# A hybrid attention and GLA layer on one core: more buffers for raw weights, deferred transposes, scalings on ScalarE, and modulation steps moved

## The chip, the cores and the metric

The kernel runs on one core of a Trainium2 chip. A core has TensorE (PE, matrix products; its weight loads are listed apart as PEld), VectorE (DVE), ScalarE (ACT), GpSimd (POOL) and SyncE (SP), which here issues most transfers. Each engine works through its own queue in order. The metric is the device time of one execution in microseconds (us).

## The reference

One layer of a diffusion backbone, batch 1, 256 latent tokens x and 256 context tokens, model width 2048, all in 32-bit floats:

```python
mod = silu(c) @ w_mod + b_mod            # 6 parts of 2048: shift1, scale1, gate1, shift2, scale2, gate2
h = rms_norm(x, g_mix) * (1 + scale1) + shift1           # the context tokens with c_ctx
qa, ka, va, qb, kb, vb, rb, lr_f, lr_b, gate_a, gate_b = split(h @ w_in)
# attention: 16 query heads, 4 key heads of 128; q and k normalised per head, rotary, window 128, sink
o_attn = softmax_with_sink(q @ k.T * 128**-0.5, [window, context]) @ v
# GLA: 4 heads (keys 256, values 512), forward and backward, decay from lr_f and lr_b
o_gla = gla_forward + gla_backward
y = sigmoid(gate_a) * (o_attn @ w_attn_o) + sigmoid(gate_b) * ((rms_norm(o_gla) * silu(rb)) @ w_gla_o)
x = x + gate1 * (y @ w_out)
h2 = rms_norm(x, g_ffn) * (1 + scale2) + shift2
a, g = split(conv3(h2 @ w_up))           # depthwise convolution over tokens, width 3; 2 x 5632 wide
out = x + gate2 * ((silu(a) * g) @ w_down)
```

## The kernel before

**Projections.** Every float matrix product is made of three products of fp32r operands: both operands are split into an upper half (hi) and the rest (lo), and hi x hi, hi x lo and lo x hi are summed. Weights are read once, in chunks of 256 rows and 512 columns (512 KB). `wload` (line 137) takes a raw buffer from the pool `wr`, which has four, and has SP load the chunk. `wsplit` (143) makes `whi` on ScalarE (line 61) and `wlo` on VectorE (line 62), each with three buffers; a raw buffer is free when wlo is made. `proj_nat` (152) gives tokens by features, 512 columns a product (lines 163 to 165), with two accumulator banks for the latent tokens or four with the context; `proj_T` (169) gives features by tokens, 256 columns a product (lines 186 to 189). There are four accumulator banks. When a block of 512 features is done, a function called evac takes the banks away.

**Work beside the projections.** Each chunk begins with a `tick` (124). It runs steps of a generator (`beside`: the GLA of a head, or an attention group) and of a list of background steps, `bg_steps`, each at a pace set by the program. The background list is the modulation of the later parts (`mod_latent`, 225): a step loads a 512 KB piece of w_mod into a raw buffer and adds two row tiles, scaled by silu(c), to a sum on VectorE (line 239, `macc`); every eighth step closes 512 columns with a transpose, a reduction and a small product (line 247, `pcl`). Parts 3, 4, 2 and 5 (shift2, scale2, gate1, gate2) are 32 steps each.

**Stages.** First the inputs are normalised, the modulation parts 0 and 1 are computed, and h is made in five groups of row tiles, with the first projections (to about 236 us). Then the four GLA heads run beside the remaining key and value projections of GLA (`gla_A`, 460; to 500). Then come the attention's keys KA and values VA (to 600; `ka_evac`, 676, normalises, rotates and transposes each bank of four heads), four query blocks QA with the attention of the group before beside each (`qa_block`, 689; `attend`, 702; to 800), the GLA output blocks RB and the merge (`rb_evac`, 784; `mg_evac`, 818; `to_T`, 776; to 1200), the output projection (`wo_evac`, 838; to about 1300), and the FFN: up-projection, convolution and down-projection in two halves (6 and 5 blocks). `norm_rope` (653) is the per-head norm: copy and square on ScalarE, sum on VectorE, `rms_scale` (276, seven tiny instructions on both), scaling and rotation on VectorE. `rows_from_cols` (257) turns a gate into rows in every partition by way of memory, with transfers on POOL's queue. The pace of background steps is 0.7 a tick during GLA, 2.0 during KA and VA, 0 during QA, 0.5 from RB on.

**What sets the order.** A scheduler orders each engine's instructions when the kernel is built, by the program's order, priorities (wsplit is preferred) and its own estimates of time, and puts in the waits. From then on every queue runs in that order.

## Time and profile before

| | |
|---|---|
| median of 3 runs | 2062.91 us (2056.2 to 2065.13) |
| the profiled execution: span, first to last instruction | 2061.8 us |
| busy: PE, PEld, DVE, ACT | 97%, 84%, 68%, 45% of the span |
| granted TensorE clock, mean | 0.990 |
| moved from and to memory | 413.71 MB, mean 201 GB/s |

For the profiled execution the profile gives the span; it lies 1.1 us under the median of the runs, and what lies around it is taken as that. The table of stages gives for each stretch the busy time of each engine with the count of its instructions, the granted clock (1.00 is full), the share of time that the 16 transfer engines were busy, and GB/s. A row of waits reads: engine, what waited, who released it, then us in total, times, and the longest. PE's busy time overstates its work, since neighbouring products overlap and a product that waits for its operand may count as busy.

### The profile page before, as it was taken

The page shows a single profiled execution, that of the slowest core. Times are in us where ns is not written, and L with a number is a line of the kernel's source. Part 1 is how long each engine was busy: PE and PEld are TensorE (multiplying, and loading weights), DVE is VectorE, ACT ScalarE, POOL GpSimd, SP SyncE. Part 2 cuts the span into 40 slices and gives each one's busy share as a digit, 9 for nine tenths or more (in the row PEclk, how much of TensorE's full clock was granted, in tenths as well). Part 3 has the DMA queues.
Part 4 walks back from the last instruction along what each step waited for, and adds up shares of the span by engine and source line. Part 5 has one row for each costly group of instructions (what it writes and reads, how often), then busy time and mean ns, then how long its engine had stood idle before and what let it go on. Part 6 is the DMA issues. An engine that isn't in the chain of part 4 may idle for free.

```text
span 2061.8 us, 30115 instructions
## 1 busy us (share of the span) xinstructions
PE 1999.2 (97%) x11792; PEld 1721.8 (84%) x11792; DVE 1405.7 (68%) x2149; ACT 937.4 (45%) x1306; POOL 41.9 (2%) x62
## 2 busy tenths in 40 slices
PE   6899999999999999999999999899999999999999
PEld 4679888888787777777787788899999889999987
DVE  4666778978867888777767665666666555666654
ACT  3323464552346665443334344554455334445533
POOL 0001100001000000000000000000000000000000
PEclk8999999999999999999999999999999999999999
DMA  9976434347664466787888875566666566666664
GB/s 347 337 247 197 120 111 123 113 118 226 213 186 114 121 194 192 254 270 260 264 279 272 294 235 184 164 184 184 184 183 184 194 193 187 184 184 183 183 209 150
DMA packets 214350, 413.71 MB, mean 201 GB/s; under 512 B 12548, under 2 KB 21092, under 8 KB 213184
## 3 DMA queue, kind: packets, MB, share of 16 engines
q1 hardware_dynamic: 212320, 406.89, 63.3%
q0 software_dynamic: 1360, 4.74, 0.8%
q8 instruction: 92, 1.51, 0.3%
q14 instruction: 50, 0.41, 0.1%
q10 hardware_dynamic: 528, 0.17, 0.0%
HBM read 409.63 MB, written 2.11 MB: 200 GB/s over the span
## 4 chain that ended last, share of the span: by engine, by line
PE 60%; issue 18%; DMA 11%; DVE 8%; ACT 2%; POOL 0%; DVEq 0%; ACTq 0%; POOLq 0%
PE acc L189 10%; PE acc L186 10%; PE acc L188 10%; PE acc L165 8%; PE acc L164 8%; PE acc L163 8%; DMA raw<-in_w_mod 8%; DVE wlo L62 3%; DVE macc L239 2%; DMA raw<-in_w_in 2%; PE pm L210 1%; PE pa L503 1%; ACT whi L61 1%; DMA raw<-in_w_gla_o 1%; PE po L589 1%
## 5 line engine op out<-in xcount | busy, mean ns | idle before, releaser
L61 ACT ACTIVATE whi<-raw 128x1024 fp32r<-128x1024 f32 x568 | 601.4, 1059 | 863.7 <-PE acc L165 366.4
L62 DVE TENSOR_TENSOR wlo<-raw,whi 128x1024 fp32r<-128x1024 f32 x568 | 693.3, 1222 | 428.3 <-ACT whi L61 422.7
L186 PE MATMUL acc<-h2h,whi 128*128 128x256 f32 x1408 | 399.5, 284 | 1.3 <-ACT h2h L346 1.3
L188 PE MATMUL acc<-h2l,whi 128*128 128x256 f32 x1408 | 399.5, 284 | 0.0
L189 PE MATMUL acc<-h2h,wlo 128*128 128x256 f32 x1408 | 399.2, 284 | 0.0
L186 PEld LDWEIGHTS acc<-h2h,whi 128*128 128x128 f32 x1408 | 271.3, 193 | 1.9 <-ACT h2h L346 1.8
L188 PEld LDWEIGHTS acc<-h2l,whi 128*128 128x128 f32 x1408 | 271.3, 193 | 0.2
L189 PEld LDWEIGHTS acc<-h2h,wlo 128*128 128x128 f32 x1408 | 271.3, 193 | 0.0
L239 DVE SCALAR_TENSOR_TENSOR macc<-raw,ccol,macc 128x512 f32<-128x512 f32 x240 | 180.6, 752 | 100.5 <-DMA raw<-in_w_mod 97.2
L163 PE MATMUL acc<-whi,h01hi 128*128 128x512 f32 x352 | 139.5, 396 | 0.9 <-ACT whi L61 0.9
L164 PE MATMUL acc<-wlo,h01hi 128*128 128x512 f32 x352 | 139.1, 395 | 1.3 <-DVE wlo L62 1.2
L163 PE MATMUL acc<-whi,h00hi 128*128 128x512 f32 x352 | 139.2, 395 | 0.0
L164 PE MATMUL acc<-wlo,h00hi 128*128 128x512 f32 x352 | 139.0, 395 | 0.2 <-DVE wlo L62 0.2
L165 PE MATMUL acc<-whi,h00lo 128*128 128x512 f32 x352 | 138.6, 394 | 0.0
L165 PE MATMUL acc<-whi,h01lo 128*128 128x512 f32 x352 | 138.2, 392 | 0.0
L163 PE MATMUL acc<-whi,ah 128*128 128x512 f32 x352 | 137.0, 389 | 0.0
L164 PE MATMUL acc<-wlo,ah 128*128 128x512 f32 x352 | 137.0, 389 | 0.0
L165 PE MATMUL acc<-whi,al 128*128 128x512 f32 x352 | 136.9, 389 | 0.0
L164 PEld LDWEIGHTS acc<-wlo,h01hi 128*128 128x128 f32 x352 | 66.4, 189 | 16.0 <-DVE wlo L62 3.2
L163 PEld LDWEIGHTS acc<-whi,h01hi 128*128 128x128 f32 x352 | 66.4, 189 | 14.3 <-ACT whi L61 1.3
L164 PEld LDWEIGHTS acc<-wlo,h00hi 128*128 128x128 f32 x352 | 66.2, 188 | 14.1 <-DVE wlo L62 1.3
L165 PEld LDWEIGHTS acc<-whi,al 128*128 128x128 f32 x352 | 66.1, 188 | 13.8
(369 smaller groups left out, 3393.2 us busy)
## 6 DMA issues: line engine op xcount, KB each, us to landing
raw<-in_w_in SPq DMA_DIRECT2D x208, 512.0 KB, 4.2
raw<-in_w_up SPq DMA_DIRECT2D x176, 512.0 KB, 3.7
raw<-in_w_mod SPq DMA_DIRECT2D x128, 512.0 KB, 3.9
raw<-in_w_down SPq DMA_DIRECT2D x88, 512.0 KB, 3.8
mraw<-in_w_mod SPq DMA_DIRECT2D x32, 1024.0 KB, 10.2
raw<-in_w_attn_o SPq DMA_DIRECT2D x32, 512.0 KB, 4.8
raw<-in_w_gla_o SPq DMA_DIRECT2D x32, 512.0 KB, 5.2
raw<-in_w_out SPq DMA_DIRECT2D x32, 512.0 KB, 3.8
```

What stands on the lines that cost most here:

```text
L61: S.activation(hi, src, AF.Copy)
L62: V.tensor_tensor(lo, src, hi.bitcast(F32), op=ALU.subtract)
L163: PE.matmul(banks[i], ahi, hi[:, k, :], start=(kt == kts[0]), stop=False)
L164: PE.matmul(banks[i], ahi, lo[:, k, :], start=False, stop=False)
L165: PE.matmul(banks[i], alo, hi[:, k, :], start=False, stop=(kt == kts[-1]))
L186: PE.matmul(o, whi, ahi, start=(kt == kts[0] and b == 0), stop=False, skip_group_check=True)
L188: PE.matmul(o, whi, alo, start=False, stop=False, skip_group_check=True)
L189: PE.matmul(o, wlo, ahi, start=False, stop=(kt == kts[-1]), skip_group_check=True)
L210: PE.matmul(a[0][q:q + 32, :], cS[:, kt, :], raw[:, k, :], start=(kt < 4), stop=(kt >= 12))
L239: V.scalar_tensor_tensor(a[0], raw[:, k, :], ccol[:, kt:kt + 1], a[0], op0=ALU.mult, op1=ALU.add)
L503: PE.matmul(pa[:, t, :], k2[:, dt, t * P:(t + 1) * P], q2[:, dt, tq * P:(tq + 1) * P], start=(dt == 0), stop=(dt == 1))
L589: PE.matmul(po, x_, y_[:, s, :], start=(n == 0), stop=(n == 11))
```

## The change

- The pool of raw weight buffers has seven instead of four.
- In both projections the products with whi of a chunk come first, for all banks, then those with wlo.
- `defer(n, fn)` puts a function on a list that `tick` empties: it runs n + 1 ticks later, first come first served. The transposes of the keys, queries, GLA outputs, merge and x1 are deferred so, as are the closing of a modulation column block and the rows of gate1. `flush` empties the list.
- A modulation step also loads the piece of the step after it. Parts 3, 4 and 2 (96 steps) run at 0.1 a tick during GLA, 1.4 during KA, 0.8 during VA, 0.51 from RB on; part 5 (32 steps) runs at 0.36 in the up-projections of the FFN's first half, and gate2's rows are made after them.
- `norm_rope` squares and sums per head on ScalarE from the accumulator bank, and scales from that bank on ScalarE: eight instructions of 128 columns in place of two of 512 on ScalarE and a reduction and a product on VectorE. The attention weights are divided by their sum on ScalarE, and the doubling of GLA's scores moves there too.
- The attention beside a query block starts later and runs faster (1.4 steps a tick from -2.9, before 0.8 from 0).
- POOL's space for transfer descriptors is set to 4096 bytes a partition, and small parameter rows use another pool.

```diff
...
     big = pool(name="big", bufs=16)
-    wr = pool(name="wr", bufs=4)
+    wr = pool(name="wr", bufs=7)
     wh = pool(name="wh", bufs=3)
...
     def columns(name, parts, eng=G):
-        rows = W2("mod", "rows", [P, P])
+        rows = sm.tile([P, P], F32, name="rows", tag="t128", bufs=2)
         n = 0
...
     beside = []
+    later = []
+    def defer(n, fn):
+        later.append([n, fn])
+    def flush():
+        while later:
+            later.pop(0)[1]()
     def tick():
+        for e in later:
+            e[0] -= 1
+        while later and later[0][0] < 0:
+            later.pop(0)[1]()
         if beside:
...
                     PE.matmul(banks[i], ahi, hi[:, k, :], start=(kt == kts[0]), stop=False)
-                    PE.matmul(banks[i], ahi, lo[:, k, :], start=False, stop=False)
-                    PE.matmul(banks[i], alo, hi[:, k, :], start=False, stop=(kt == kts[-1]))
+                    PE.matmul(banks[i], alo, hi[:, k, :], start=False, stop=False)
+            for i, l in enumerate(lhs):
+                for k in range(nk):
+                    kt = k0 + k
+                    PE.matmul(banks[i], l(kt)[0], lo[:, k, :], start=False, stop=(kt == kts[-1]))
         for i in range(len(lhs)):
...
             hi, lo = wsplit(w[k0 * P:(k0 + nk) * P, c0:c0 + 512])
-            for f in range(4):
-                for k in range(nk):
...
-                        PE.matmul(o, whi, ahi, start=(kt == kts[0] and b == 0), stop=False,
-                                  skip_group_check=True)
-                        PE.matmul(o, whi, alo, start=False, stop=False, skip_group_check=True)
-                        PE.matmul(o, wlo, ahi, start=False, stop=(kt == kts[-1]), skip_group_check=True)
+            for part in range(2):
+                for f in range(4):
+                    for k in range(nk):
+                        kt = k0 + k
+                        w_ = (lo if part else hi)[:, k, f * P:(f + 1) * P]
+                        for i, r in enumerate(rhs):
+                            b = (f % per) if n == 1 else i
+                            o = banks[f // per][:, b * T:(b + 1) * T]
+                            ahi, alo = r(kt)
+                            PE.matmul(o, w_, ahi, start=(kt == kts[0] and b == 0 and part == 0),
+                                      stop=(kt == kts[-1] and part == 1), skip_group_check=True)
+                            if part == 0:
+                                PE.matmul(o, w_, alo, start=False, stop=False, skip_group_check=True)
         for i in range(len(banks)):
...
         return [lambda k0=k0: step(k0) for k0 in range(0, KT, nk)]
-    def mod_latent(part, j, dst):
-        a = []
-        c0 = part * D + j * 512
-        def step(k0):
+    def mod_latent(parts):
+        seq = [(part, dst, j, k0) for part, dst in parts for j in range(4) for k0 in range(0, KT, 2)]
+        raws, a = {}, []
+        def get(i):
+            if i < len(seq) and i not in raws:
+                part, _, j, k0 = seq[i]
+                c0 = part * D + j * 512
+                raws[i] = wload(w_mod[k0 * P:k0 * P + 256, c0:c0 + 512])
+        def step(i):
+            part, dst, j, k0 = seq[i]
+            get(i)
+            get(i + 1)
             if k0 == 0:
-                a.append(W2("mod", "macc", [P, 512]))
-            raw = wload(w_mod[k0 * P:k0 * P + 256, c0:c0 + 512])
+                a[:] = [W2("mod", "macc", [P, 512])]
+            raw = raws[i]
             for k in range(2):
...
                 V.tensor_reduce(rs, tr, op=ALU.add, axis=AX.X)
...
+                def out():
...
+                defer(3, out)
+        return [lambda i=i: step(i) for i in range(len(seq))]
     def rows_from_cols(name, col):
...
                           start=(dt == 0), stop=(dt == 1))
-        V.tensor_scalar(at, pa, 2.0, None, op0=ALU.mult)
+        S.activation(at, pa, AF.Copy, scale=2.0)
         def halves(x, m):
...
         return vh, vl
-    for part, dst in ((3, shift2), (4, scale2), (2, gcol1), (5, gcol2)):
-        for j in range(4):
-            bg_steps.extend(mod_latent(part, j, dst))
-    bg_rate[:] = [0.7, 0.0]
+    bg_steps.extend(mod_latent(((3, shift2), (4, scale2), (2, gcol1))))
+    bg_rate[:] = [0.1, 0.0]
     qbt = M("qb", [P, 8, T])
...
         y = W2("fc", "y", [P, 4, P])
-        S.activation(y, b.rearrange("p (h d) -> p h d", h=4), AF.Copy)
         sq = W2("fc", "sq", [P, 512])
-        S.activation(sq, y.rearrange("p h d -> p (h d)"), AF.Square)
         s4 = sm.tile([P, 4], F32, name="s4", tag="s4")
-        V.tensor_reduce(s4, sq.rearrange("p (h d) -> p h d", h=4), op=ALU.add, axis=AX.X)
+        for h in range(4):
+            S.activation(sq[:, h * P:(h + 1) * P], b[:, h * P:(h + 1) * P], AF.Square, accum_out=s4[:, h:h + 1])
         r4 = rms_scale(s4, HD, [P, 4])
-        V.tensor_tensor(y, y, r4.unsqueeze(2).to_broadcast([P, 4, P]), op=ALU.mult)
+        for h in range(4):
+            S.activation(y[:, h, :], b[:, h * P:(h + 1) * P], AF.Copy, scale=r4[:, h:h + 1])
         z = sq.rearrange("p (h d) -> p h d", h=4)
...
         z = norm_rope(b, rk if i < 2 else None, i % 2)
-        pt = bank("ptk", (P, 4, P))
-        for h in range(4):
-            PE.transpose(pt[:, h, :], z[:, h, :], ident)
-        split(kTh[:, :, i * P:(i + 1) * P], kTl[:, :, i * P:(i + 1) * P], pt)
-    bg_rate[0] = 2.0
+        def turn():
+            pt = bank("ptk", (P, 4, P))
+            for h in range(4):
+                PE.transpose(pt[:, h, :], z[:, h, :], ident)
+            split(kTh[:, :, i * P:(i + 1) * P], kTl[:, :, i * P:(i + 1) * P], pt)
+        defer(2 + i, turn)
+    bg_rate[0] = 1.4
     proj_nat(w_in, 0, KA, ALL, h_xc, ka_evac)
+    bg_rate[0] = 0.8
     vah, val = v_block(VA, "va")
...
             z = norm_rope(b, rq, t)
...
+            defer(2 + t, turn)
         proj_nat(w_in, 0, QA + g * 512, ALL, h_x, evac)
...
             for h in range(4):
-                V.tensor_scalar(sc[h], sc[h], ds_[:, h:h + 1], None, op0=ALU.mult)
+                S.activation(sc[h], sc[h], AF.Copy, scale=ds_[:, h:h + 1])
             yield
...
     for g in range(4):
-        beside[:] = [attend(g, qTs), 0.8, 0.0]
+        beside[:] = [attend(g, qTs), 1.4, -2.9]
         qTs = qa_block(g + 1) if g < 3 else ga_block()
...
         beside.clear()
-    bg_rate[0] = 0.5
+    bg_rate[0] = 0.51
     glan = W2("fb", "glan", [P, 512])
...
             V.tensor_tensor(s_, s_, o_, op=ALU.mult)
-            to_T(s_, gh, gl, j, t)
+            defer(1 + t, lambda: to_T(s_, gh, gl, j, t))
         proj_nat(w_in, 0, RB + j * 512, ALL, h_x, rb_evac)
...
             V.tensor_tensor(a2[t], a2[t], a1[t], op=ALU.add)
-            to_T(a2[t], mh, ml, j, t)
+            defer(1 + t, lambda: to_T(a2[t], mh, ml, j, t))
         proj_nat(A["w_gla_o"][0], 0, j * 512, ALL, [tok(gh, gl, 0), tok(gh, gl, 1)], mg_evac)
...
         S.preload_act_table_set("natural_log_exp_and_others")
-    while bg_steps:
-        bg_steps.pop(0)()
+    assert not bg_steps
     x1 = [M(f"x1_{t}", [P, D]) for t in range(2)]
...
         nc.sync.dma_start(x1[t], A["x"][0][t * P:(t + 1) * P, :])
-    gate1 = rows_from_cols("gate1", gcol1)
+    gate1 = []
+    defer(4, lambda: gate1.append(rows_from_cols("gate1", gcol1)))
     x1T = [M(f"x1T{i}", [P, 8, T]) for i in range(2)]
...
             y = W2("fc", "yo", [P, 512])
-            V.tensor_tensor(y, b, gate1[:, js], op=ALU.mult)
+            V.tensor_tensor(y, b, gate1[0][:, js], op=ALU.mult)
             V.tensor_tensor(x1[t][:, js], x1[t][:, js], y, op=ALU.add)
             S.activation(y, x1[t][:, js], AF.Square, accum_out=ss1[:, t, j:j + 1])
...
+            defer(1 + t, turn)
         proj_nat(A["w_out"][0], 0, j * 512, ALL, [tok(mh, ml, 0), tok(mh, ml, 1)], wo_evac)
+    flush()
     s1 = sm.tile([P, 2], F32, name="s1", bufs=1)
...
                      scale2[:, kt:kt + 1], shift2[:, kt:kt + 1])
-    gate2 = rows_from_cols("gate2", gcol2)
+    bg_steps.extend(mod_latent([(5, gcol2)]))
+    bg_rate[:] = [0.36, 0.0]
     h2 = [lambda kt: (h2h[kt // 8][:, kt % 8, :], h2l[kt // 8][:, kt % 8, :])]
...
             proj_T(w_up, DFF + j * 512, ALL, h2, lambda p_, b: up_evac(p_, b, 1))
+        if half == 0:
+            assert not bg_steps
+            flush()
+            gate2 = rows_from_cols("gate2", gcol2)
         for j in range(4):
-            def dn_evac(t, b, j=j, half=half):
+            def dn_evac(t, b, j=j, half=half, gate2=gate2):
                 js = slice(j * 512, (j + 1) * 512)
...
     from concourse.bass_utils import run_bass_kernel_spmd
-    nc = bacc.Bacc("TRN2", target_bir_lowering=False, num_devices=1)
+    nc = bacc.Bacc("TRN2", target_bir_lowering=False, num_devices=1,
+                   dynamic_dma_scratch_size=4096)
     arrays, aps = {}, {}
```

43 lines of the change are left out of this document (19 added, 24 removed).

## The prediction

> **What bounds the kernel now.** I read the page first, then stages of the span, then the same stages for the projection matmuls alone (tile acc), then the waits.
>
> ```profile
> span 2061.8 us, 30115 instructions
> PE 1999.2 (97%) x11792; PEld 1721.8 (84%) x11792; DVE 1405.7 (68%) x2149; ACT 937.4 (45%) x1306; POOL 41.9 (2%) x62
> 50.00:100.00 50.00, 44.65 (x322) 32.19 (x315) 31.71 (x67) 18.43 (x30) 0.00 (x0) 0.96 0.91 335
> 236.00:500.00 264.00, 258.52 (x1424) 222.96 (x1423) 220.96 (x418) 144.39 (x291) 28.51 (x35) 1.00 0.44 129
> 500.00:600.00 100.00, 95.64 (x420) 77.83 (x419) 72.66 (x125) 31.91 (x44) 0.00 (x0) 0.97 0.68 207
> 600.00:800.00 200.00, 199.15 (x932) 156.32 (x932) 168.84 (x351) 119.27 (x212) 0.58 (x1) 1.00 0.53 155
> 800.00:1200.00 400.00, 384.12 (x1688) 307.77 (x1687) 297.23 (x379) 164.03 (x172) 0.00 (x0) 1.00 0.81 266
> 1290.00:1330.00 40.00, 33.78 (x216) 30.84 (x215) 28.74 (x55) 20.78 (x36) 1.06 (x2) 0.87 0.54 162
> 1350.00:1400.00 50.00, 50.00 (x419) 50.00 (x419) 30.30 (x38) 24.03 (x30) 0.00 (x0) 1.00 0.66 185
> 1600.00:1650.00 50.00, 50.00 (x222) 41.41 (x221) 24.85 (x23) 19.25 (x19) 0.00 (x0) 1.00 0.60 194
> ```
>
> Columns: stage, its length, busy time (count) of PE, PEld, DVE, ACT, POOL, granted clock, DMA share, GB/s. The last two rows are the unit prices: a 256-column projection matmul takes 50/419 = 0.119 us, a 512-column one 50/222 = 0.225 us, when nothing waits. A busy share of 97% hides waits, so I count matmuls instead.
>
> ```profile
> 236.00:500.00 264.00, 192.40 (x956) 157.23 (x955) 7.93 (x12) 9.41 (x16) 1.00 0.44 129
> 500.00:600.00 100.00, 93.92 (x398) 75.40 (x397) 2.75 (x4) 4.76 (x8) 0.97 0.68 207
> 600.00:800.00 200.00, 147.79 (x578) 106.60 (x578) 0.00 (x0) 7.07 (x12) 1.00 0.53 155
> 800.00:1200.00 400.00, 378.28 (x1614) 300.76 (x1613) 8.96 (x14) 11.75 (x20) 1.00 0.81 266
> 236.00:500.00 264.00, 29.72 (x104) 19.82 (x104) 1.00 0.44 129
> 253.82 0.89 PE pa L503 x8
> 283.90 3.69 PE pa L568 x16
> 546.01 0.60 PE L680 MATMUL ptk<-ident,sq 128*128 128x128 f32 x4
> ```
>
> - Merge stage (800 to 1200): 1614 x 0.225 = 363 us; the other 74 are 56 transposes, at most 0.15 each (the last row), and 18 tiny ones: some 8. About 29 us lost, the largest sum.
> - Keys (500 to 600): 398 x 0.225 = 90, and 22 small ones, 2: 8 lost.
> - Attention (600 to 800): 578 + 192 (scores and values, 512 columns) x 0.225 = 173; 160 transposes cost up to 24: 3 to 13 lost.
> - GLA (236 to 500): the fifth row is line 188, a third of the 256-column ones: 312 x 0.119 + 644 x 0.225 = 182; 112 more of 512 columns 25, 288 at 0.111 (line 503) 32, 64 at 0.231 (line 568) 15: 254. About 10 lost.
> - FFN (from 1330): nothing lost. Its DVE stands at 61%, DMA at 0.66.
>
> Who is late in the merge stage:
>
> ```profile
> SPq L68 <- DVE wlo L62: 201.3, 134, 4.4
> SPq L68 <- DVE macc L239: 73.1, 65, 2.1
> DVE macc L239 <- DMA raw<-in_w_mod: 67.9, 44, 3.4
> PEld acc L164 <- DVE wlo L62: 11.4, 17, 2.4
> PEld pto L779 <- DVE m L820: 7.3, 6, 2.6
> ```
>
> It is one ring. SP holds each load back until VectorE frees one of four raw buffers; the w_mod rows then land late; VectorE stands 67.9 us in front of them, with wlo and the merge sums queued behind; TensorE waits for those.
>
> **The change part by part.** Instruction counts: TensorE's are the same. The profiled span is 1.1 us under the median of the runs (2062.9); I add that at the end.
>
> *Seven buffers, w_mod loaded one step ahead, whi products before wlo products, transposes deferred (merge).* The rate of steps stays (0.5 to 0.51 a tick, about 75 steps), so VectorE has the same work; what goes is its standing still. Without the loss the stage moves 266 x 400 us in 371 us, 287 GB/s; the row 50:100 shows 335, so the transfers allow it. A step's load is now issued a whole step earlier, two ticks or 24 matmuls x 0.225 = 5.4 us, more than the 3.4 us longest wait. The transposes go behind 12 to 24 matmuls, 2.7 to 5.4 us against waits of 2.6 us. wlo is asked for 8 matmuls (1.8 us) later in a chunk, against 2.4. Bounds: 28 us gained to 5 lost (a w_mod buffer held longer takes slots from weights). I take 23, since each wait named is covered.
>
> *w_mod steps out of GLA.* 32 ticks x 0.7 = 22 steps become 3. A step is two products:
>
> ```profile
> L239 DVE SCALAR_TENSOR_TENSOR macc<-raw,ccol,macc x122: 740/751/755, 799.7 to 1190.6; 128x512 f32<-128x512 f32 x122
> PEld pa L503 <- DVE q L523: 3.8, 4, 1.3
> ```
>
> 19 x 1.5 = 28 us of VectorE's 221 go, and their 19 loads from SP. Of the 10 us lost there 3.8 are TensorE's waits for decay factors from VectorE (second row); the rest stands at the heads' ends, whose chains remain, with their ScalarE steps. 0 to 9 gained; I take 6. The doubled scores (4 instructions) to ScalarE: nothing, ScalarE is at 55%.
>
> *Head norms on ScalarE, transposes deferred (keys).*
>
> ```profile
> 540.52 1.11 PE L680 MATMUL ptk<-ident,sq 128*128 128x128 f32 x4 [4.36 <-DVE sq L671]
> 537.00:540.00 3.00, 0.00 (x0) 0.00 (x0) 3.00 (x11) 0.00 (x0) 0.00 (x0) 0.76 0.79 298
> 540.00:545.00 5.00, 4.48 (x13) 3.71 (x14) 3.74 (x9) 2.49 (x4) 0.00 (x0) 0.50 0.38 104
> L656 ACT ACTIVATE y<-acc x12: 573/597/601, 524.9 to 711.9; 128x512 f32<-128x512 f32 x12
> L658 ACT ACTIVATE sq<-y x12: 614/632/635, 525.5 to 712.5; 128x512 f32<-128x512 f32 x12
> L727 ACT ACTIVATION_READ_ACCUMULATOR s<-s,mx 128x1 f32 x32 | 5.9, 186 | 0.0
> L282 ACT ACTIVATE rstd<-msq x16: 186/196/205, 15.7 to 1303.6; 128x4 f32<-128x4 f32 x12, 128x2 f32<-128x2 f32 x3, 128x8 f32<-128x8 f32 x1
> L660 DVE TENSOR_REDUCE s<-sq x12: 677/680/686, 530.8 to 716.2; 128x4 f32<-128x512 f32 x12
> L662 DVE TENSOR_TENSOR y<-y,rstd x12: 681/684/691, 537.0 to 728.4; 128x512 f32<-128x512 f32 x12
> ```
>
> Now TensorE stands 4.4 us before the first key transpose, and the clock falls to 0.50 afterwards (some 2.5 us more). Deferral removes that wait. But the accumulator bank is freed later: before, one 0.60 us copy; after, only when the last scaled copy has read it. A ScalarE instruction of 128 columns lies between 0.20 (4 columns) and 0.63 (512), in proportion 0.30. The chain: 4 x (0.30 + 0.19) squares, 1.2 for seven tiny steps, 4 x 0.30 copies, 0.4 for crossings: 4.8 us a bank. In the built order ScalarE runs the four chains one behind the other, and V's projection, next on TensorE, needs all four banks. Its queue does 9 matmuls for bank 0, then waits for bank 1. Bank 0 ends 1.4 us before the block: waits of 4.8 - 1.4 = 3.4, then 2.8 (4.8 less 9 x 0.225), then about 1 and 1: 8 us, and perhaps the clock. So one wait of 7 goes, one of 8 to 11 comes. Bounds 6 gained to 12 lost; I take 2 lost.
>
> The Trainium skill (TensorE: Matmul & The Clock Gate, Part 1) says that the clock halves after an idle window of about 3.4 us and recovers after as long a busy one. The trace agrees, with 0.50 behind a wait of 4.36 us. By that rule a first wait of 3.4 us may fall on either side; with half speed for 3.4 us the term would be 1.7 us worse.
>
> *Attention.* 8 norms each save VectorE 0.68 + 0.68 us; 32 scalings move as well:
>
> ```profile
> L732 DVE TENSOR_SCALAR s<-s,ds x32: 473/482/489, 627.4 to 789.9; 128x512 f32<-128x512 f32 x32
> L727 ACT ACTIVATE s<-s,mx 128x512 f32<-128x512 f32 x32 | 22.7, 709 | 0.0
> ```
>
> VectorE: 169 - 11 - 14 = 144 of 200. ScalarE: 119 + 8 x (3.2 - 1.2) + 32 x (0.60 to 0.71) = 154 to 158 of 200. Neither is full, but ScalarE runs whi in the same queue. The query transposes come at the third and fourth tick (5 us of matmuls or more), the attention starts at tick 3 and runs 1.4 steps a tick. 10 gained to 10 lost; I take 4 gained.
>
> The Trainium skill (ScalarE: Activation LUTs, Rules for kernel authors) says to use VectorE, not ScalarE, for a multiplication. The trace agrees on the single instruction (0.48 against 0.60 to 0.71 us); the stage as a whole is the rival below.
>
> *w_mod part 5 to the FFN's first half.* 32 steps over 96 ticks of 2.9 us: VectorE gets 32 x 1.5 + four closings (some 3 us each) = 60 us on 276, from 61 to 83%; DMA from 0.66 to 0.66 x 1.36 = 0.90. The merge stage ran at 0.81 with losses, but with four buffers. 0 to 48 lost (each product wholly in the way); I take 2. The cover is ScalarE and VectorE being a chunk ahead.
>
> *Start.* The row 50:100 is near the transfer limit (0.91), with 5 us of PE idle. More buffers let SP issue earlier: 3 gained; bounds 8 gained to 8 lost.
>
> *Late wlo products bring the banks of a four-bank block to their end together*, 1.4 us before the block's end for the first instead of 4 us. Some 16 such blocks, 0 to 0.7 us each (one VectorE evacuation of 0.68): I take 2 lost.
>
> *Gate rows.*
>
> ```profile
> dgate<-row POOLq DMA_DIRECT2D x2, 8.0 KB, 1.9
> gate<-dgate POOLq DMA_DIRECT2D x2, 1024.0 KB, 6.6
> L426 POOL DMA_DIRECT2D wlr<-in_w_in x1: 1217/1217/1217, 167.1 to 167.1; - x1
> L433 PE MATMUL plr<-h00hi,wlr x16: 379/379/403, 222.7 to 224.7; 128*32 128x256 f32 x16
> ```
>
> gate1 is now begun at the fifth tick of the output projection: 8.5 us of transfers on POOL's queue against 4 chunks x 2.7 = 10.8 us. It costs nothing while that cover holds; beyond it VectorE would wait with wlo behind. gate2 leaves the turn to the FFN: 1 gained. POOL's smaller descriptor space: nothing; of its loads wlr, in the most and smallest pieces, is issued at 167 and first used at 223 (last rows).
>
> Sum: -23 - 6 + 2 - 4 + 2 - 3 + 2 - 1 = -31: span 2031, median about 2032 us.
>
> **The rivals.**
> - *Everything recovered* (all of GLA's and merge's loss, 38; keys 6, attention 10, start 8; no new cost): 2001 us. For it: the ring explains almost all. Against: the four bank chains.
> - *ScalarE becomes the limit in keys and attention.* For it: 154 to 158 of 200 us in one queue, whi behind 0.7 us instructions. If half of its 37 new us falls on the path, 4 gained turns into 18 lost: 2054.
> - *The buffers do nothing*, because the merge is limited by transfers at 266 GB/s: 23 gone, 2055. Against: 335 in the row 50:100.
> - *The FFN loses what it had for nothing* (slower). VectorE at 83%: a w_mod product or its late load in front of wlo stalls TensorE, in a stage where nothing is idle. At the full 1.5 us a step 48 us, 2032 - 2 + 48 = 2078. It ends the gain at 1.0 us a step; the merge stage lost 29/75 = 0.4 a step, all causes together, which speaks against it.
>
> **How the numbers follow.** A measurement of this kernel can tell about 0.5% (10 us) from no change. Chances: forecast 0.48 (own range 2015 to 2047), all recovered 0.20, ScalarE 0.12, buffers 0.10, FFN 0.10. Faster than 2052.6: the first two, some of ScalarE's and of the buffers' cases, 0.78; within: 0.12; slower: 0.10. The range from 2000 to 2062 leaves out the FFN case and the tail below full recovery.
>
> **What would show it.** Right: in the merge, macc's wait for w_mod falls from 67.9 to under 15 us and matmuls per 50 us rise from 202 to about 217 (1614 in 372 us); no wait at ptk, but one of 3 us or more at the first matmul of V's projection, released by ScalarE; FFN chunks still at 419 matmuls per 50 us. Wrong: SP still waiting for wlo most of the merge; TensorE waiting for whi in the attention; fewer than 410 matmuls per 50 us in the first FFN half.

## The result: 0.35% slower, with no gain where most of it was expected

The changed kernel takes 2069.85 us (median; 2066.69 to 2072.24), the kernel before in the same rounds 2062.94 (2056.2 to 2065.13): a ratio of 1.0035, 95% interval 1.0023 to 1.0047. That is slower by less than the 0.5% which the prediction takes as its bound, and 8 us above the upper end of its range. First the page after (head and busy times) and the stages as the prediction shows them for before (length, busy time and count of PE, PEld, DVE, ACT, POOL, granted clock, DMA share, GB/s):

```profile
span 2066.3 us, 30147 instructions
PE 2002.2 (97%) x11792; PEld 1728.7 (84%) x11792; DVE 1372.9 (66%) x2089; ACT 965.0 (47%) x1462; POOL 39.6 (2%) x62
```

```profile
50.00:100.00 50.00, 47.22 (x330) 36.10 (x326) 31.39 (x67) 18.50 (x30) 0.00 (x0) 0.95 0.98 357
236.00:500.00 264.00, 257.92 (x1404) 221.98 (x1403) 196.76 (x364) 145.65 (x295) 26.26 (x35) 0.99 0.33 97
500.00:600.00 100.00, 95.55 (x414) 77.12 (x413) 43.74 (x76) 35.89 (x84) 0.00 (x0) 0.97 0.42 125
600.00:800.00 200.00, 199.16 (x929) 155.78 (x928) 151.92 (x307) 144.18 (x321) 0.00 (x0) 1.00 0.54 161
800.00:1200.00 400.00, 385.58 (x1705) 313.36 (x1704) 294.47 (x372) 166.32 (x177) 0.58 (x1) 0.98 0.81 266
1350.00:1400.00 50.00, 50.00 (x418) 49.84 (x418) 37.41 (x56) 23.92 (x29) 0.00 (x0) 1.00 0.73 237
```

VectorE's work moved as intended: 24 us out of GLA, 29 out of the keys, 17 out of the attention, 7 more per 50 us in the FFN. But the merge shows the same 266 GB/s and 0.81 as before.

A window cuts through stages: RB begins at 738 us in both kernels and the merge at 853, so the window 800 to 1200 holds 53 us of RB. I therefore also divided each trace at the start of the n-th projection matmul, n being the sum of each stage's matmuls (384 + 384 + 192 for the start, 384 for the second keys block of GLA (KB1), 576 for its values V1 to V3, and so on; 1440 for the merge). Durations in us; the columns after "after" are experiments, told below. From the end of the table's last row to the last projection matmul it is 469.6 or 469.7 us in all.

| stage | before | after | 7 buffers in before | no gate pieces | old order | held everywhere | before, 4 held | before, 7 held | held from merge on |
|---|---|---|---|---|---|---|---|---|---|
| start | 217.9 | 213.7 | 220.1 | 213.5 | 215.8 | 212.9 | 216.5 | 215.8 | 214.2 |
| KB1 | 75.6 | 80.3 | 68.3 | 77.1 | 76.1 | 77.1 | 76.3 | 77.9 | 80.7 |
| V1 to V3 (GLA) | 191.2 | 191.2 | 195.1 | 191.3 | 180.5 | 191.0 | 190.6 | 190.7 | 191.1 |
| KA and VA | 97.2 | 97.8 | 111.0 | 97.6 | 103.0 | 97.5 | 110.8 | 99.7 | 97.7 |
| QA and GA0 (attention) | 156.0 | 155.3 | 156.4 | 155.5 | 156.4 | 155.4 | 158.3 | 158.3 | 155.4 |
| RB | 114.9 | 114.3 | 117.3 | 114.4 | 116.3 | 135.5 | 113.3 | 110.9 | 114.2 |
| merge | 355.0 | 353.8 | 354.5 | 333.6 | 349.6 | 333.3 | 345.5 | 333.6 | 333.3 |
| output | 100.2 | 102.1 | 100.3 | 101.5 | 103.5 | 100.6 | 100.7 | 100.2 | 101.0 |
| FFN, first up half | 279.0 | 282.1 | 279.2 | 280.2 | 284.3 | 280.8 | 278.5 | 279.3 | 279.5 |

The waits of the merge after (engine, what waited, releaser; us, times, longest; 800 to 1200 us):

```profile
DVE macc L266 <- DMA raw<-in_w_mod: 77.9, 43, 4.1
DVE macc L264 <- DMA raw<-in_w_mod: 5.6, 7, 2.4
SPq L68 <- DVE wlo L62: 180.9, 133, 4.5
SPq L68 <- DVE macc L266: 78.0, 60, 1.6
PE pto L817 <- DVE m L858: 11.8, 3, 5.4
```

VectorE's wait for the w_mod pieces (gate pieces from here on) has grown, from 70.3 us (67.9 of them on the line that the prediction shows) to 83.5, where the prediction asked for under 15. SP's largest wait is still that for wlo, 180.9 of 400 us (before 201.3); the prediction had named this, "most of the merge", as a sign of being wrong. Two cuts of the timeline show why, first VectorE's queue, then SP's:

```profile
1008.49 1.54 DVE L266 SCALAR_TENSOR_TENSOR macc<-raw,ccol,macc 128x512 f32<-128x512 f32 x2 [1.61 <-DMA raw<-in_w_mod]
1009.94 2.35 DVE L62 TENSOR_TENSOR wlo<-raw,whi 128x1024 fp32r<-128x1024 f32 x2
1014.38 1.54 DVE L266 SCALAR_TENSOR_TENSOR macc<-raw,ccol,macc 128x512 f32<-128x512 f32 x2 [2.08 <-DMA raw<-in_w_mod]
```

```profile
1004.63 0.37 SPq L68 DMA_DIRECT2D raw<-in_w_mod  x1
1005.77 1.50 SPq L68 DMA_DIRECT2D raw<-in_w_in  x2
1010.06 0.37 SPq L68 DMA_DIRECT2D raw<-in_w_mod  x1
```

The products on one piece end at 1008.49 + 1.54 = 1010.03; at 1010.06 SP issues the next piece, into the buffer just freed; it is there 4.3 us later, and VectorE, which has only two wlo (2.35 us) in between, stands 2.08 us. One turn takes 1014.38 - 1008.49 = 5.89 us, and in it come two weight chunks, worth 24 x 0.225 = 5.4 us to TensorE. As an estimate from this one turn, 61 turns (0.51 a tick, 120 ticks) x 0.49 us are 30 us; the merge's loss is some 20 (the experiments). So the gate pieces are in effect single-buffered, seven buffers or four.

In the queues this can be counted. SP takes buffers in the order of its loads; VectorE frees them in the order of its own queue, where the scheduler has put each gate product ahead of weight chunks loaded before it. In the merge, from the VectorE instruction that frees a gate piece's buffer to the piece's own product there are 3 places in both kernels (most pieces; a place is one chunk or piece). For weight chunks it is 4 or 5 before and mostly 9 after: the three new buffers hold weights which wait for room in whi and wlo. The median time from a gate piece's load to its product did not move either: 4.2 us before and 4.2 after.

### The profile page after: what moved, and what is told of

Same layout as the page of the kernel before. It is cut to its first block, busy times and chain, and to the rows that moved or that the text cites. A ratio compares the mean times of both kernels' runs of the same rounds, so it can differ in the third digit from the quotient of the medians.

```text
span 2066.3 us, 30147 instructions
## 1 busy us (share of the span) xinstructions
PE 2002.2 (97%) x11792; PEld 1728.7 (84%) x11792; DVE 1372.9 (66%) x2089; ACT 965.0 (47%) x1462; POOL 39.6 (2%) x62
## 4 chain that ended last, share of the span: by engine, by line
PE 63%; issue 19%; DMA 8%; DVE 7%; ACT 3%; POOL 0%; DVEq 0%; ACTq 0%; POOLq 0%
PE acc L203 19%; PE acc L176 10%; PE acc L177 10%; PE acc L206 10%; PE acc L181 9%; DMA raw<-in_w_mod 7%; DVE wlo L62 2%; DVE macc L266 2%; PE pm L227 1%; PE pa L534 1%; PE po L620 1%; ACT whi L61 1%; PE pa L599 1%; ACT gm L509 0%; PE pto L817 0%
## 5 line engine op out<-in xcount | busy, mean ns | idle before, releaser
L203 PE MATMUL acc<-h2h,whi 128*128 128x256 f32 x1408 | 347.3, 284 | 1.5 <-ACT h2h L377 1.5
L206 PE MATMUL acc<-h2l,whi 128*128 128x256 f32 x1408 | 346.8, 284 | 0.0
L203 PE MATMUL acc<-h2h,wlo 128*128 128x256 f32 x1408 | 198.7, 284 | 0.7 <-DVE wlo L62 0.6
L203 PEld LDWEIGHTS acc<-h2h,wlo 128*128 128x128 f32 x1408 | 182.3, 193 | 1.3 <-DVE wlo L62 1.3
L181 PE MATMUL acc<-wlo,h00hi 128*128 128x512 f32 x352 | 98.7, 397 | 0.0
L181 PE MATMUL acc<-wlo,h01hi 128*128 128x512 f32 x352 | 96.9, 393 | 0.2 <-DVE wlo L62 0.2
L181 PE MATMUL acc<-wlo,ah 128*128 128x512 f32 x352 | 94.1, 389 | 0.0
L176 PEld LDWEIGHTS acc<-whi,h00hi 128*128 128x128 f32 x352 | 68.3, 194 | 20.2 <-ACT y L691 5.3
L177 PEld LDWEIGHTS acc<-whi,h00lo 128*128 128x128 f32 x352 | 68.4, 194 | 12.9
L181 PEld LDWEIGHTS acc<-wlo,ah 128*128 128x128 f32 x352 | 66.1, 188 | 13.8
```

The source lines that it names most:

```text
L176: PE.matmul(banks[i], ahi, hi[:, k, :], start=(kt == kts[0]), stop=False)
L177: PE.matmul(banks[i], alo, hi[:, k, :], start=False, stop=False)
L181: PE.matmul(banks[i], l(kt)[0], lo[:, k, :], start=False, stop=(kt == kts[-1]))
L203: PE.matmul(o, w_, ahi, start=(kt == kts[0] and b == 0 and part == 0), stop=(kt == kts[-1] and part == 1), skip_group_check=True)
L206: PE.matmul(o, w_, alo, start=False, stop=False, skip_group_check=True)
```

## The experiments

### Whose buffers: a ring for the gate pieces, four buffers, seven in the kernel before

**Own ring**, the changed kernel with three buffers for gate pieces alone and four for weights:

```diff
-    wr = pool(name="wr", bufs=7)
+    wr = pool(name="wr", bufs=4)
...
+    def mload(src):
+        raw = wr.tile([P, 2, 512], F32, name="modraw", tag="modraw", bufs=3)
...
-                raws[i] = wload(w_mod[k0 * P:k0 * P + 256, c0:c0 + 512])
+                raws[i] = mload(w_mod[k0 * P:k0 * P + 256, c0:c0 + 512])
```

> Edit: the changed kernel with the modulation's pieces of w_mod in three buffers of their own, the weights in four (seven in all, as in the changed kernel). Theory A (in the merge the load of a w_mod piece waits for the buffer that the piece before it has just left, so VectorE stands for a whole transfer in each step, with three buffers more or without): the pieces are loaded earlier, VectorE's wait for w_mod in the merge falls from 83.5 us (77.9 and 5.6) to under 40, the merge blocks from 354 us to under 342, the kernel 10 to 25 us faster than the changed one. Theory B (the transfers are at their limit in the merge): the wait stays above 70 us and the time within 5 us of the changed kernel. Theory C (four buffers are too few for the weights): slower than the changed kernel by 5 us or more.

**Four buffers**, the changed kernel with the first pair of lines alone:

> Edit: the changed kernel with four raw buffers again, all else as changed. Theory A: the three buffers went to weights that wait for room behind them; the merge blocks stay within 5 us of 354 and the kernel within 8 us of the changed one. Theory B (transfers at their limit): the same. Rival (the seven buffers do give the merge something, which another part of the change takes away): the merge 10 to 20 us longer, the kernel 10 to 25 us slower.

**Seven in before**, the kernel before with `wr` of seven (and, to make room, the smaller descriptor space and the rows' other pool):

```diff
-    wr = pool(name="wr", bufs=4)
+    wr = pool(name="wr", bufs=7)
```

> Edit: the kernel before with seven raw buffers (and the room made for them by the smaller descriptor space and the other pool for parameter rows), nothing else. Theory A: in the merge the same loop, 355 us within 5; VectorE still waits 60 to 85 us for w_mod there; some 3 to 5 us gained in the first 220 us, the kernel 0 to 6 us faster than before. Rival (seven buffers alone remove the merge's waits, and the later parts of the change bring them back): 15 us or more faster than before.

Measured: own ring 2105.38 us, ratio 1.0210 [1.0195, 1.0225]; four buffers 2077.41, 1.0079 [1.0060, 1.0098]; seven in before 2070.79, 1.0051 [1.0033, 1.0069]. Own ring, TensorE's first wait from 0 to 260 us and VectorE's waits from 850 to 1205:

```profile
PE pm L232 <- DMA mraw<-in_w_mod: 33.4, 7, 11.7
...
DVE wlo L62 <- ACT whi L61: 31.9, 27, 1.6
DVE macc L271 <- DMA modraw<-in_w_mod: 28.6, 21, 3.0
```

The merge fell to 334.2, but the scheduler, free to load gate pieces at once, put 31 of them ahead of the start's last weight load; the start took 266.6 us instead of 213.7. Seven buffers in the kernel before left the merge at 354.5 and cost 14 us in KA and VA. Four in the changed one made its merge 363.7 and V1 to V3 200.9: there I had expected the merge within 5 us of 354, and it came 9.9 longer, nearly the rival's 10 to 20. So three more shared buffers do not help the merge of the kernel before, while the changed kernel, which asks for its gate pieces one step ahead, loses by having only four. Which part of the change makes it need them was not separated.

### Without the gate pieces

The kernel leaves out 7 of 8 w_mod loads and all products but the first of each column block in parts 3, 4, 2 and 5, so their sums hold one row tile of sixteen:

```diff
-            get(i)
-            get(i + 1)
             if k0 == 0:
+                get(i)
...
-            raw = raws[i]
+            raw = raws[i - i % 8]
...
+                if kt:
+                    continue
```

> Edit: the changed kernel with seven of eight loads and all but the first product of each modulation column block left out (shift2, scale2, gate1 and gate2 are then sums over one row tile alone, so the time is that of a kernel with less work). Theory A: what the merge loses hangs on the w_mod pieces: the merge blocks fall from 354 to 326 to 334 us (15 blocks of 96 products at 0.226 us are 325), the first FFN half from 282 to 279, the kernel 25 to 38 us faster than the changed one. Rival (the losses are the transposes' and the merge sums' own chains): the merge stays above 345 us, the kernel less than 12 us faster.

Measured: 2041.6 us, 0.9901 [0.9884, 0.9918], merge 333.6. So what the merge loses hangs on the gate pieces. This doesn't tell whether their transfers or their place is at fault.

### Own buffers, loaded late

Two own buffers, five for weights, and each gate load placed on SP behind the weight load before it in the program:

```diff
+        d = load(raw, src.rearrange("(c p) d -> p c d", p=P))
+        tc.add_manual_dep(d, last_w[0].name, mybir.DependencyInfo(
+            mybir.DependencyClass.NoSync, mybir.DependencyReason.DATA), reason="order of loads")
```

> Edit: the changed kernel with two buffers for the modulation's pieces and five for the weights, and each load of a piece kept on SyncE's queue behind the load of weights that stands before it in the program. Theory A (the merge waits because a w_mod piece is asked for only when the one before it is used up; the own buffers of the first experiment cost their 53 us at the start because nothing held the pieces back there): start within 3 us of 214, merge 330 to 340 us instead of 354, first FFN half 278 to 281 instead of 282, the kernel 14 to 26 us faster than the changed one (2044 to 2056 us). Rival (the gain of the first experiment's merge came from pieces done ahead in earlier stages, not from the order of waiting): the merge stays above 348 us, the kernel within 6 us of the changed one.

Measured: 2057.79 us, 0.9990 [0.9979, 1.0002]; start 212.2, merge 348.0. VectorE still waited (800 to 1200):

```profile
DVE macc L275 <- DMA modraw<-in_w_mod: 69.2, 42, 4.1
```

The start was mended, the merge gained only 6 us, and the 330 to 340 expected were missed. The pieces had 4 to 7 places, and 6.9 us (median) from load to product. But each load now stood on SP right behind weight loads, and took 6.8 us to land (median from 855 to 1195 us; 4.0 in the changed kernel): the lead that the places gave went into the landing.

### One part undone: keys' norm, product order, deferral

The changed kernel with the old `norm_rope`; with the product order of before; and with `defer` running its function at once:

```diff
-        for h in range(4):
-            S.activation(sq[:, h * P:(h + 1) * P], b[:, h * P:(h + 1) * P], AF.Square, accum_out=s4[:, h:h + 1])
...
+        S.activation(y, b.rearrange("p (h d) -> p h d", h=4), AF.Copy)
```

> Edit: the changed kernel with the head norm as it was before (copy and square of 512 columns on ScalarE, sum and scaling on VectorE), transposes still deferred. Theory D (the wait of 3.9 us and the slow clock at the start of V's projection come from the four norm chains that hold the banks): no wait there, keys and values 97.8 us to 90 to 93; the attention, with more on VectorE, 0 to 4 us longer; the kernel 3 to 8 us faster than the changed one. Rival (the chains of VectorE take over): keys and values stay above 96 us, the kernel the same or slower.

```diff
-            for i, l in enumerate(lhs):
-                for k in range(nk):
-                    kt = k0 + k
-                    PE.matmul(banks[i], l(kt)[0], lo[:, k, :], start=False, stop=(kt == kts[-1]))
...
+                    PE.matmul(banks[i], ahi, lo[:, k, :], start=False, stop=False)
```

> Edit: the changed kernel with the three products of each tile in the order of before (whi, wlo, whi). If the new order gives TensorE room against late wlo, the merge gets 3 to 8 us longer and the kernel 3 to 10 us slower than the changed one. If the new order costs at the ends of the four-bank blocks, start, GLA and keys together get 3 to 8 us shorter. Forecast: within 5 us of the changed kernel, both being small.

```diff
-        later.append([n, fn])
+        fn()
```

> Edit: the changed kernel with nothing deferred: transposes, closings and gate rows stand where their data are made, as before. Theory A: deferring by one chunk did not remove the waits at the merge's transposes (three of 3.2 to 5.5 us, where VectorE stands before w_mod); without it the merge stays within 6 us of 354, the keys gain a wait at ptk of 2 to 5 us; the kernel 0 to 8 us slower than the changed one. Rival (the scheduler's estimates already place the transposes, and a deferred one only comes out of step): 3 us or more faster.

Measured: old norm 2065.22 us, 1.0028 [1.0017, 1.0038], KA and VA 91.2 instead of 97.8; old order 2061.33, 1.0008 [0.9997, 1.0019]; no deferral 2072.17, 1.0059 [1.0042, 1.0076], merge 355.0, KA and VA 98.9. Against the changed kernel's 1.0035, deferral is worth some 5 us of the whole (the two intervals overlap a little). In KA and VA the new norm takes back what the deferral brings: 97.2 us before, 91.2 with deferral and the old norm, 97.8 with both new; of these 6.6 us the whole shows about 1.4, less than the 3 to 8 expected. With the old order V1 to V3 take 180.5 instead of 191.2, but KA then 55.1 instead of 48.0 and the FFN half 2 more; V1 to VA together go from 289.0 to 283.5. In the merge TensorE then waits for wlo (800 to 1200):

```profile
PE acc L177 <- DVE wlo L62: 6.5, 12, 1.8
```

### The place in VectorE's queue

The hold: the first product of a gate piece may not stand in VectorE's queue ahead of the lower half made last before it in the program. As a rule that is the wlo of the weight chunk before it; but `split` makes every lower half, those of the attention and of the transposes too. The hold adds no wait on a semaphore; it only takes an order away from the scheduler. In the merge the gate pieces then have 7 places in before with seven buffers, mostly 9 in after, and 4 in before with four buffers.

```diff
-        V.tensor_tensor(lo, src, hi.bitcast(F32), op=ALU.subtract)
+        last_lo[:] = [V.tensor_tensor(lo, src, hi.bitcast(F32), op=ALU.subtract).ins]
...
+                if k == 0 and last_lo:
+                    tc.add_manual_dep(m.ins, last_lo[0].name, mybir.DependencyInfo(
+                        mybir.DependencyClass.NoSync, mybir.DependencyReason.DATA), reason="order")
```

It was put into the changed kernel, and into the kernel before with four and with seven buffers. Beside them ran the three own buffers with no gate load before the last load of the start (`start_last` saved from the chain of loads):

> The changed kernel with its seven shared buffers; the only edit is that the first product of each w_mod piece may not stand in VectorE's queue ahead of the subtraction (wlo) of the weight chunk before it in the program. The number of VectorE's instructions on loaded pieces between the one that frees a gate piece's buffer and that piece's product rises from 3 to 7 to 9. Theory A (the place in VectorE's queue makes the gate pieces single-buffered): VectorE's wait for w_mod in 800 to 1200 us, 83.5 us, falls below 30; the merge, 353.8 us, takes 330 to 340; the whole kernel 2045 to 2056. Rival B (the merge has not enough transfer rate for weights and gate pieces together): the wait moves to wlo, the merge stays at 345 to 358 and the whole at 2060 to 2072. Rival C (holding VectorE's products back delays wlo elsewhere): the merge falls, and V's and the keys' stages or the up half pay it back, whole above 2060.

> The kernel before with its four shared buffers; the only edit is the same hold of each w_mod product behind the wlo before it. Its count rises from 3 to 4. Theory A: one place more is about 2.7 us more time for a 4.3 us transfer, so the merge falls from 355.0 us to 335 to 348 and the whole by 5 to 20, to 2040 to 2056. Rival B (transfer rate): merge 352 or more, the whole within 5 of 2060. If four buffers held do as well as seven held, the buffers were not needed at all.

> The kernel before with seven shared buffers and the hold; with seven buffers and no hold the merge took 354.5 us and the whole 2070.8. The count rises from 3 to 7 to 9. Theory A: merge 330 to 340, the whole 2045 to 2058, the difference to the four held buffers in the merge below 8. Rival B: merge 350 or more, the whole 2065 or more.

> The changed kernel with three buffers of their own for the w_mod pieces and four for the weights (as in the experiment with own buffers), but no w_mod piece may be issued before the last load of the start. Theory A: the start is back at 213 us (266.6 with own buffers alone), the merge at 334, the up half at 278, the whole at 2038 to 2050. Rival B (the fast merge came from pieces that had been loaded during the slow start): the merge goes back to 345 or more and the whole to 2055 or more.

Measured, ratio to before and merge:

| | as scheduled | held |
|---|---|---|
| before, 4 buffers | 1, 355.0 | 1.0022 [1.0008, 1.0037], 345.5 |
| before, 7 buffers | 1.0051 [1.0033, 1.0069], 354.5 | 0.9906 [0.9889, 0.9923], 333.6 |
| after, 7 buffers | 1.0035 [1.0023, 1.0047], 353.8 | 1.0014 [1.0004, 1.0024], 333.3 |

Buffers alone and place alone each make the kernel before slower; the two together make it 0.94% faster (2042.96 us). In before with seven held, 800 to 1200: the stage, then VectorE's first wait and TensorE's only one.

```profile
800.00:1200.00 400.00, 398.91 (x1792) 326.86 (x1791) 314.12 (x395) 173.81 (x182) 1.07 (x2) 1.00 0.85 280
```

```profile
DVE wlo L62 <- ACT whi L61: 78.0, 65, 1.9
...
PE pto L783 <- DVE sr L793: 1.0, 1, 1.0
```

No wait for w_mod is left, and the median time from a gate piece's load to its product is 10.8 us (14.8 in after, held from the merge on), though as many bytes are moved, and faster than the 266 GB/s of before: the rival "transfers limit the merge" falls. VectorE still stands 78 us, now for ScalarE's whi; but its wlo are done 2.9 us or more before TensorE's first product with them, more than a chunk's 12 x 0.225 = 2.7 us, and that standing costs nothing. With four buffers held, VectorE's wait for w_mod is down to 4.4 us as well, and yet the merge takes 345.5: the other 12 us, which seven buffers bring, are not that wait, and what they are was not followed up.

In the changed kernel the merge's 20 us came, and RB's stage took 21 of them back. Held everywhere, SP's first wait from 755 to 805 us, and two neighbours in VectorE's queue:

```profile
SPq L69 <- DVE macc L267: 29.7, 3, 27.3
```

```profile
794.52 0.69 DVE L62 TENSOR_TENSOR ol<-poa,oh 128x512 fp32r<-128x512 f32 x1 [1.45 <-ACT oh L61]
795.13 0.74 DVE L267 SCALAR_TENSOR_TENSOR macc<-raw,ccol,macc 128x512 f32<-128x512 f32 x1
```

Gate pieces were loaded during the last attention block, but their products stood behind that block's long chain in VectorE's queue; so SP could not load RB's weights, and the block's tail ran with nothing beside it. By 769.5 us seven gate pieces (not two, as the first expectation of the next section has it) were issued and none of them used, so all seven buffers were taken. The hold itself put them there: by the program's paces a step falls into RB's first tick, where the lower half made last is not a wlo but ol, the output of that attention block. In before with seven held, whose first such step comes in the second tick, RB took 110.9. Rival C's kind of loss was right, in a stage that I had not named. In before with four held it was KA and VA (110.8).

Own buffers after the start: 2059.71, 0.9987 [0.9975, 1.0000], merge 334.2 and start 213.6, as expected; but V1 to V3 took 202.7 and the output 106.8, with four buffers for the weights. My 2038 to 2050 for the whole missed that.

### The hold from the merge on, and what adds to it

```diff
-                if k == 0 and last_lo:
+                if k == 0 and hold:
...
+    hold.append(1)
     sig = []
```

The hold is switched on where the merge begins and stays on, so that it also covers the FFN's pieces.

> The changed kernel with the hold of the w_mod products behind the wlo before them in the merge alone (with the hold everywhere RB's stage took 135.5 us, because two gate pieces that were already loaded stood in VectorE's queue behind the last attention block, and SyncE waited 27.3 us for their buffers). Theory A (the loss against the forecast is the place in the queue and nothing else in the merge): RB is back at 113 to 117 us, the merge takes 332 to 340, the whole 2044 to 2053. Rival B (RB's loss has another cause): RB stays above 125 and the whole at 2058 or more. Rival C (the merge's gain is returned in the output product or the up half): the merge falls, but the out and up1 stages together rise from 384 us by 8 or more.

With the old keys' norm, and with the old product order:

> As the hold in the merge, and the keys' norm as before the change (one copy, one square, sum and scaling on VectorE). If the keys' term (6 us with the old norm in the changed kernel) and the merge's are independent: KA and VA together 90 to 93 us instead of 97.8, the merge 332 to 340, the whole 2038 to 2047. If one returns the other, the whole is that of the hold alone within 2.

> As the hold in the merge, and the product order of before (whi for one tile, wlo, whi). Alone this order took V1-3 from 191.2 to 180.5, KA from 48.0 to 55.1 and the whole from 2069.9 to 2061.3, and the merge from 353.8 to 349.6. If it adds to the hold: the whole 2036 to 2046. If the merge's share of it was the same wait for gate pieces, the merge is that of the hold alone within 3 and the whole 2040 to 2048. If the order with wlo between makes PE wait for VectorE once the gate pieces no longer wait, the merge is 340 or more.

Measured: 2043.11 us, 0.9921 [0.9905, 0.9938]; with the old norm 2040.92, 0.9909 [0.9895, 0.9924]; with the old order 2039.73, 0.9905 [0.9890, 0.9920]. The merge is 333.3 in all three, RB 114.2 in the first. The stage of the first:

```profile
800.00:1200.00 400.00, 400.00 (x1804) 327.71 (x1803) 311.83 (x391) 176.48 (x188) 1.10 (x2) 1.00 0.82 276
```

1804 matmuls against 1705, with TensorE waiting for nothing that the view of waits shows. This one ordering edit is worth 24 us (the spans 2066.3 and 2042.7; the ratios 1.0035 and 0.9921 say the same), and these versions beat both kernels. The 4 us that the old order alone had won in the merge (349.6) are not added to the hold's. With the old norm KA and VA fall by 6.5 us to 91.2, but RB grows by 3.1, and the whole is 2.2 us lower: about as much as the expectation took for no gain at all.

Last, the old norm with no gate piece before KB1's end, and the old norm with the old order:

```diff
-    bg_rate[:] = [0.1, 0.0]
+    bg_rate[:] = [0.0, 0.0]
...
     a, kb1 = with_gla(0, kbt, kb_block)
+    bg_rate[:] = [0.12, 0.0]
```

> The hold in the merge and the old keys' norm, and no w_mod piece before the end of the second keys' block (the rate of the background steps is 0 there and 0.12 instead of 0.1 in V's). Theory (KB1's 4.7 us are PE's wait for wgl and the lower clock behind it, because VectorE stood before the first w_mod pieces): KB1 74 to 77 us instead of 80.4, the whole 3 to 5 below the kernel without this edit (2040.9), 2035 to 2039. Rival (the new product order in the groups ahead moved work into KB1): KB1 stays at 79 to 81 and the whole within 2 of 2040.9.

> The hold in the merge, the old keys' norm and the old product order together. If the two add: 2040.9 and 2039.7 alone, so 2035 to 2039 together, with V1-3 at 180.5 and KA at 50 to 53. If GLA's gain with the old order is only moved into KA, whatever the norm: V1-3 and KA together 234 to 237 as with the order alone (235.8), the whole 2038 to 2042.

Measured: 2041.28 us, 0.9910 [0.9887, 0.9932]; and 2041.47, 0.9906 [0.9891, 0.9921]. KB1 fell from 80.4 to 77.3, close to what the theory said (74 to 77), but the whole did not follow, and the two old parts do not add: V1 to V3 and KA took 234.3, yet nothing remained. With the hold alone RB begins at 739.0 us and ends at 853.2. In the last four kernels it begins at 731.8, 734.6, 726.7 and 728.9 and ends at 849.0, 850.0, 848.8 and 849.0: what is saved ahead of RB beyond some 4 us is returned in RB. From 725 us on TensorE waits for the lower halves of the attention weights (ptl, 3.3 to 4.3 us in the three with the old norm) and for the GLA output (sr, up to 2.9 us). Which of VectorE's work comes late there was not tried and stays open.

## Why the prediction was wrong

*Merge, -23: the step that failed.* Measured -1.2. The size was right: with the hold the stage takes 333.3, 22 less than before. What failed is the sentence "A step's load is now issued a whole step earlier, two ticks or 24 matmuls". That holds in the program's order. In the queues three places stayed three, each load still waited for the product ahead of it, and the time from load to product stayed at 4.2 us (median) where the sentence promised 5.4 more. The prediction read from the queues what each engine does, not how far each load stands from its use. "It is one ring" was right; more buffers in one ring lengthen the lead of those who use it in order, here the weights, and not of a user that jumps the queue. The Trainium skill (Perfetto Trace Analysis, Identifying Performance Opportunities) says that a gap that repeats on the engine that should be saturated can mean too little room for the next tile, and names the buffer count. Here that is half of it: in the kernel before, seven for four changed the merge by 0.5 us alone (354.5 against 355.0), and by 12 once the order was held (333.6 against 345.5).

*Rivals.* "The buffers do nothing" (2055) was right about the merge's gain, for a wrong reason, as the 276 to 280 GB/s of the held kernels show. The FFN's 2078 was nearer as a number, by luck: its stall did not happen. Its half lost 3.1 us (2 predicted), with 416 projection matmuls in 50 us against 419, and the pieces cost 0.5 in the kernel held from the merge on.

*GLA, -6.* Measured 0.0: VectorE's 24 us left and TensorE's waits stayed. From 236 to 500 us after:

```profile
PE pa L599 <- DVE kf L592: 4.1, 4, 1.1
PE pa L534 <- DVE q L554: 1.9, 4, 0.5
```

Before it was 3.2 and 2.3 at the same two places. The first stands near each head's end (at 283.5, 347.6, 411.4 and 475.7 us), where the prediction had named the chains as remaining; the second is the wait for decay factors, all that it had reason to expect gone, and it stayed too. Its rows gave 3.8 us there, and it took 6. What did count in this stage was the product order: the old one gives 180.5 there and returns 7 of the 10.7 in KA.

*KB1, not in the sum, and the start, -3.* The start gained 4.2 us and KB1 lost 4.7: together they take 293.4 us before and 294.0 after. VectorE meets gate pieces at the start of GLA, before as well as after, and the product that makes wgl, for which KB1's GLA waits, stands behind them, so that it runs at 232.5 us in both kernels, whatever the start gained. After the change (the waits from 200 to 250 us, then a window of 10 us):

```profile
DVE macc L264 <- DMA raw<-in_w_mod: 4.3, 1, 4.3
DVE macc L266 <- DMA raw<-in_w_mod: 3.6, 1, 3.6
PE pz L504 <- DVE wgl L478: 2.1, 1, 2.1
```

```profile
230.00:240.00 10.00, 7.90 (x50) 7.45 (x49) 5.06 (x7) 5.88 (x10) 0.73 (x1) 0.83 0.22 65
```

TensorE waits for wgl, and the clock is 0.83 in those 10 us. Without those pieces (the run with none before KB1's end) KB1 was 3.1 shorter. In the kernels held everywhere and with the old order wgl happens to stand ahead of the pieces, and KB1 takes 77.1 and 76.1, with that wait gone; so some 3 to 4 of the 4.7 us hang on this wait.

*Keys, +2.* Right in kind: +0.6, and the new wait is where it was put, 3.91 us before V's first matmul (3.4 predicted; of the 2.8, 1 and 1 that were to follow, TensorE's waits show none), released by ScalarE's copy of the bank, while ptk's wait is gone (the timeline, then 3 us of windows):

```profile
528.54 0.26 ACT L688 ACTIVATE sq<-acc 128x128 f32<-128x128 f32 x1
532.07 1.14 ACT L691 ACTIVATE y<-acc,rstd 128x128 f32<-128x128 f32 x4 [0.82 <-DVE rstd L318]
533.26 0.80 PE L176 MATMUL acc<-whi,h00hi 128*128 128x512 f32 x1 [3.91 <-ACT y L691]
```

```profile
533.00:536.00 3.00, 2.74 (x7) 2.19 (x8) 2.58 (x8) 1.65 (x11) 0.00 (x0) 0.50 0.25 97
```

From the first square to the end of the copies it is 533.21 - 528.54 = 4.7 us (4.8 predicted). Behind a wait of 3.91 us the clock is 0.50, as it was behind 4.36 before. With the old norm behind the same deferral the stage shows what was given away (500 to 600 us, old norm in the changed kernel, 444 matmuls against 414):

```profile
500.00:600.00 100.00, 99.45 (x444) 80.58 (x443) 51.72 (x88) 34.56 (x50) 0.00 (x0) 1.00 0.44 139
```

*The rest.* Attention -0.7 (-4 predicted, inside its bounds); ScalarE reached 144 of 200 us, not 154 to 158, VectorE 152 instead of 144, and the rival of a limiting ScalarE did not happen. Late banks, +2 predicted: the old order takes 5.5 us less from V1 to VA, where five of the 16 blocks stand, and 2.1 more in the start; so at least from V1 to VA the term was too small. Output +1.9, for which the sum had nothing; from 1200 to 1320 us VectorE shows no wait for gate1's rows, so its cause is open. The sum was -31 and came out at +4.5 in the span; of the 35 between, the merge is 22, GLA 6, KB1 5, the attention 3.

## What to carry to other kernels

Where two users share a ring of buffers, count in the queues as built, for each of them, how many instructions lie between the one that frees its buffer and its own use; more buffers help a user only if that count grows. A scheduler may move a cheap product forward into a gap and so make its next load late: pinning its order, with no new wait, was worth 24 us here, where three more buffers alone were worth nothing to the kernel before. Look at what the pin ties to in each stage: tied to the end of a long dependent chain, the same pin held SP up for 27 us and gave the gain back.

## What was not expected of the hardware

A gate piece took 4.3 us from issue to its product with the transfer engines at 0.81, so even one gate piece in flight at a time all but kept pace; the loss was 0.5 us in the turn shown. ScalarE's squares of 128 columns took 0.26 to 0.32 us and each was followed by a read of the sum of 0.19 to 0.25 us. The scaling of 512 columns took 0.71 us on ScalarE, against 0.48 on VectorE before.
